# Turning x at stage borders: the norm weights applied in place in PSUM, the two parts taken four blocks at a time

## The chip, the core and the metric

The kernel runs on one core of one Trainium2 chip. The metric is the device time of one execution in microseconds (us). Before the change it is 942.28 us, the median of three runs (942.03 to 942.88).

The core's engines work side by side and meet through semaphores. TensorE (PE in the profile, with PEld for its weight loads) multiplies matrices and writes to PSUM, VectorE (DVE) and ScalarE (ACT) do elementwise work, GpSimd (POOL) does a little of it, and SyncE (SP) starts transfers.

## The reference

The kernel computes a two-layer encoder on x, 256 tokens by 1024 features. Each layer is

```
x += 0.5 * swiglu(rms_norm(x, ffn1_norm), ...)
x += mixer(rms_norm(x, mix_norm))
x += 0.5 * swiglu(rms_norm(x, ffn2_norm), ...)

rms_norm(x, g) = x * rsqrt(mean(x*x) + 1e-6) * g
swiglu(h, w_gate, w_up, w_down) = (silu(h @ w_gate) * (h @ w_up)) @ w_down
```

The mixer of the first layer holds global and windowed attention side by side; that of the second is a two-dimensional neighbourhood attention. A last norm follows. That makes six stages in a row, numbered 0 to 5: feed-forward, even mixer, feed-forward, feed-forward, odd mixer, feed-forward. Everything is float32.

## The kernel before, in words

**Three products for one.** Each float32 matrix is split into a high part in the reduced format fp32r and a low part, the rest. A product is then high times high, high times low and low times high: `mm` (lines 471 to 473) issues these three matmuls for each piece of weight, in that order: x's high part against the weight's high part (L471), x's high part against the weight's low part (L472), x's low part against the weight's high part (L473). ScalarE makes high parts (`high_part`, L479, a plain copy into fp32r) and VectorE low parts (`low_part`, L482, source minus high part). Both do so for all weights as well, which come by DMA into three raw buffers and are split some way ahead of their use into seven buffers.

**Turned x.** A matmul needs x with features on the partitions. x lies in two tiles of 128 tokens (tt = 0 and 1) by 1024 features. When a stage ends, each half row of x, 512 features, gets its last addition from VectorE (`add_to_x`, L614). Then `after` (L1392) spawns the task `prepare` (L521) for that token tile and half, and for the second half also `row_rstd` (L494), which sums the squares on ScalarE (L500, two passes) and has 1/sqrt taken. The norm's row factor is applied later, behind the matmul; the norm's weights, one for each feature, are applied while x is turned, where features lie on partitions and a weight is one scalar per partition.

`prepare` works in three steps. In the first, TensorE transposes four blocks of 128 by 128 into one PSUM bank (L527; the tag is `tp`, and there are two such banks). In the second, ScalarE makes four high parts, each by one instruction that reads a block, multiplies by the weights and writes to SBUF (`part_h`, L512; the profile calls these tiles `th`). In the third, VectorE makes four low parts, each by one instruction that reads the block again, multiplies again and takes the high part off (`part_l`, L517; tiles `tl`). I call such a set of four blocks a group. There are four groups at each border (two token tiles with two halves) and five borders, so 20 groups. Stage 0 turns its x by other code (`first_gates`), which uses `part_h` and `part_l` too.

**The order of the work.** Each engine runs its instructions in the order in which the program issues them; nothing reorders them. The program is a main line of matmuls in which every three matmuls (`mm`) are followed by a `tick` (L274). A tick advances the tasks: each `yield n` in a task means that its next step is issued n ticks later. A tick also lets the weight splitting go on, at a rate that is a table's entry for each stage. So where an instruction stands in ScalarE's or VectorE's queue is fixed by ticks that were counted when the program was built, not by what happens on the chip.

At a border the matmuls of the next stage begin with token tile 0, block by block through its eight blocks of 128 features (`project`, L602), then token tile 1. The program starts a token tile's when the steps of both its groups have all been issued (`ready`, L535). A group of the second half is thus first used by the fifth block of its `project`. In the feed-forward stages, `x_sums` (L727) also adds high and low parts together again (L738).

Of the kernel before, what the change touches and what calls it, by code (L numbers as in the profile page):

```python
# [10 lines left out]
F32R = mybir.dt.float32r  # L11
BF16 = mybir.dt.bfloat16
U16 = mybir.dt.uint16
AF = mybir.ActivationFunctionType
# [4 lines left out]
P = 128  # L19
# [3 lines left out]
KD = D // P  # L23
# [182 lines left out]
class Trunk:  # L206
# [287 lines left out]
    def row_rstd(self, tt, dest):  # L494
# [8 lines left out]
        nc.vector.tensor_tensor(s, ss[:, 0:1], ss[:, 1:2], op=ALU.add)  # L503
        dest[tt] = self.rstd(s, 1, D)[:, 0:1]

    def part_h(self, tb, tt, i, k, j):

        if (i, tt) not in self.hts:
            self.hts[i, tt] = [self.one.tile([P, KD, P], F32R, tag=f"hT{tt}{p}", name=self.name(f"t{p}")) for p in "hl"]
        hi, lo = (t[:, k, :] for t in self.hts[i, tt])  # L510
        gain = self.gains[:, i * KD + k : i * KD + k + 1]
        self.nc.scalar.activation(hi, tb[:, j * P : j * P + P], AF.Copy, scale=gain)  # L512
        return hi, lo
# [7 lines left out]
    def prepare(self, tt, i, half, dest):  # L521

        nc = self.nc
        tb = self.bank("tp")
        for j in range(4):
            b = half * 4 + j
            nc.tensor.transpose(tb[:, j * P : (j + 1) * P], self.x[tt][:, b * P : (b + 1) * P], self.ident)  # L527
        yield 1
        his = [self.part_h(tb, tt, i, half * 4 + j, j) for j in range(4)]
        yield 1  # L530
        for j, hl in enumerate(his):
            self.part_l(tb, tt, i, half * 4 + j, j, hl)
        dest += his

    def ready(self, tt):  # L535

# [1029 lines left out]
```

## Time and profile before

| of the profiled execution | value |
|---|---|
| its own time | 942.26 us |
| span of its instructions | 940.5 us |
| TensorE busy | 921.8 us, 98% |
| VectorE busy | 783.1 us, 83% |
| ScalarE busy | 677.8 us, 72% |
| GpSimd busy | 91.9 us, 10% |
| high parts of turned x, L512, by ScalarE | 96 instructions |
| low parts of turned x, L517, by VectorE | 96 instructions |
| transposes of x in `prepare`, L527 | 80 instructions |

Of the 96, 80 belong to `prepare` and 16 to stage 0. A line of the grouped view names the source line, the engine, the operation, what it writes and reads, the shape and the count; then the busy time and the mean in ns of one; then the time that the engine stood idle just before such instructions and what ended that. A line of the timeline gives start and length in us, and a number in brackets is idle time before it. Where several equal instructions follow each other they are one line with "x4", and its length runs from the first start to the last end. Matmuls are pipelined: one of 512 columns is shown with 0.39 us, but the next one starts about 0.227 us after it.

### The profile page before, as it was taken

The page shows a single profiled execution, that of the slowest core. Times are in us where ns is not written, and L with a number is a line of the kernel's source. Part 1 is how long each engine was busy: PE and PEld are TensorE (multiplying, and loading weights), DVE is VectorE, ACT ScalarE, POOL GpSimd, SP SyncE. Part 2 cuts the span into 40 slices and gives each one's busy share as a digit, 9 for nine tenths or more (in the row PEclk, how much of TensorE's full clock was granted, in tenths as well). Part 3 has the DMA queues.
Part 4 walks back from the last instruction along what each step waited for, and adds up shares of the span by engine and source line. Part 5 has one row for each costly group of instructions (what it writes and reads, how often), then busy time and mean ns, then how long its engine had stood idle before and what let it go on. Part 6 is the DMA issues. An engine that isn't in the chain of part 4 may idle for free.

```text
span 940.5 us, 12389 instructions
## 1 busy us (share of the span) xinstructions
PE 921.8 (98%) x4399; PEld 752.7 (80%) x4399; DVE 783.1 (83%) x1212; ACT 677.8 (72%) x1091; POOL 91.9 (10%) x152
## 2 busy tenths in 40 slices
PE   9999999999999999999999999999999999999997
PEld 6887888877878787888888878778878788878886
DVE  6799778778869989889978897989767687987897
ACT  7678975467787778875657778657877577769753
POOL 1300000064410000000100000008030000000001
PEclk9999999999999999999999999999999999999999
DMA  8857875554326577767466877575534358487851
GB/s 298 278 171 247 250 233 194 184 150 109 101 91 200 201 236 228 236 210 252 151 186 221 201 234 229 202 251 172 167 104 136 133 180 246 137 255 228 219 224 45
DMA packets 129343, 183.16 MB, mean 195 GB/s; under 512 B 50688, under 2 KB 63744, under 8 KB 129280
## 3 DMA queue, kind: packets, MB, share of 16 engines
q1 hardware_dynamic: 128704, 181.58, 61.2%
q10 hardware_dynamic: 576, 0.79, 0.2%
q8 instruction: 34, 0.56, 0.2%
q14 instruction: 29, 0.24, 0.1%
HBM read 169.76 MB, written 1.05 MB: 182 GB/s over the span
## 4 chain that ended last, share of the span: by engine, by line
PE 66%; DVE 16%; ACT 10%; issue 4%; DMA 3%; POOL 0%; SPq 0%; POOLq 0%; ACTq 0%; DVEq 0%
PE pj L471 9%; PE pj L472 9%; PE pj L473 9%; PE s L472 9%; PE s L473 9%; PE s L471 9%; DVE lo L482 7%; ACT hi L479 3%; DMA glu<-turned 2%; ACT turned L560 2%; DVE raw L395 2%; PE o L1040 2%; ACT shi L479 2%; PE tp L1117 1%; PE o L472 1%
## 5 line engine op out<-in xcount | busy, mean ns | idle before, releaser
L482 DVE TENSOR_TENSOR lo<-raw,hi 128x1024 fp32r<-128x1024 f32 (+1 forms) x372 | 376.1, 1031 | 78.5 <-ACT hi L479 77.0
L479 ACT ACTIVATE hi<-raw 128x1024 fp32r<-128x1024 f32 (+1 forms) x372 | 318.7, 889 | 50.3 <-DMA raw<-in_ffn_w_up 13.8
L471 PE MATMUL pj<-hi,th 128*128 128x512 f32 x367 | 146.7, 400 | 0.9 <-ACT glu L766 0.9
L472 PE MATMUL s<-lo,th 128*128 128x512 f32 x373 | 145.5, 390 | 1.0 <-DVE lo L482 1.0
L472 PE MATMUL pj<-lo,th 128*128 128x512 f32 x367 | 143.9, 392 | 2.6 <-DVE lo L482 2.3
L471 PE MATMUL s<-hi,th 128*128 128x512 f32 x373 | 146.2, 392 | 0.0
L473 PE MATMUL s<-hi,tl 128*128 128x512 f32 x373 | 145.3, 390 | 0.0
L473 PE MATMUL pj<-hi,tl 128*128 128x512 f32 x367 | 143.3, 390 | 0.0
L472 PEld LDWEIGHTS pj<-lo,th 128*128 128x128 f32 x367 | 69.1, 188 | 17.9 <-DVE lo L482 5.5
L472 PEld LDWEIGHTS s<-lo,th 128*128 128x128 f32 x373 | 70.1, 188 | 16.4 <-DVE lo L482 2.1
L473 PEld LDWEIGHTS s<-hi,tl 128*128 128x128 f32 x373 | 70.0, 188 | 14.5
L471 PEld LDWEIGHTS s<-hi,th 128*128 128x128 f32 x373 | 70.1, 188 | 14.4
L471 PEld LDWEIGHTS pj<-hi,th 128*128 128x128 f32 x367 | 69.0, 188 | 15.4 <-ACT glu L766 1.3
L473 PEld LDWEIGHTS pj<-hi,tl 128*128 128x128 f32 x367 | 68.9, 188 | 14.5
L491 POOL TENSOR_TENSOR rstd<-var,mhalf 128x1 f32<-128x1 f32 (+2 forms) x16 | 17.1, 1070 | 593.7 <-ACT th L512 314.4
L560 ACT COPY turned<-glu 128x1024 uint16<-128x1024 uint16 (+1 forms) x48 | 60.1, 1251 | 9.7 <-DMA glu<-turned 9.7
L479 ACT ACTIVATE shi<-raw 128x1024 fp32r<-128x1024 f32 x30 | 31.8, 1059 | 42.4 <-DVE raw L395 26.1
L556 ACT COPY turned<-glu 128x1024 uint16<-128x1024 uint16 (+1 forms) x48 | 46.4, 966 | 21.1 <-DVE glu L794 14.8
L471 PE MATMUL s<-hi,g_h 128*128 128x512 f32 (+1 forms) x131 | 51.4, 392 | 0.0
L473 PE MATMUL s<-hi,g_l 128*128 128x512 f32 (+1 forms) x131 | 50.9, 388 | 0.0
L472 PE MATMUL s<-lo,g_h 128*128 128x512 f32 (+1 forms) x131 | 50.8, 388 | 0.0
L479 ACT ACTIVATE shi<-two 128x1024 fp32r<-128x1024 f32 x30 | 31.7, 1057 | 19.2 <-DVE two L395 19.1
(482 smaller groups left out, 1677.3 us busy)
## 6 DMA issues: line engine op xcount, KB each, us to landing
raw<-in_ffn_w_down SPq DMA_DIRECT2D x44, 1024.0 KB, 5.1
raw<-in_ffn_w_up SPq DMA_DIRECT2D x28, 1024.0 KB, 5.3
raw<-in_ffn_w_gate SPq DMA_DIRECT2D x26, 1024.0 KB, 5.0
raw<-in_ffn_w_gate SPq DMA_DIRECT2D x35, 512.0 KB, 4.1
raw<-in_ffn_w_up SPq DMA_DIRECT2D x32, 512.0 KB, 5.1
raw<-in_odd_w_qkv SPq DMA_DIRECT2D x12, 1024.0 KB, 5.1
raw<-in_even_w_in SPq DMA_DIRECT2D x4, 1024.0 KB, 5.1
raw<-in_even_w_out SPq DMA_DIRECT2D x8, 512.0 KB, 5.8
```

The costliest lines, as they stand in the source:

```text
L395: add = lambda o, x, y: self.nc.vector.tensor_tensor(o, x, y, op=ALU.add)
L471: mm(ps, h, wh, start=first, stop=False)
L472: mm(ps, h, wl, start=False, stop=False)
L473: mm(ps, l, wh, start=False, stop=last)
L479: self.nc.scalar.activation(hi, src, AF.Copy)
L482: self.nc.vector.tensor_tensor(lo, src, hi.bitcast(F32), op=ALU.subtract)
L491: nc.gpsimd.tensor_tensor(r[:, :n], v[:, :n], self.mhalf[:, :n], op=ALU.pow)
L556: self.nc.scalar.copy(planes.rearrange("p (h c) -> p h c", h=2), back.rearrange("p (c h) -> p h c", h=2))
L560: self.nc.scalar.copy(planes.rearrange("p (c h) -> p h c", h=2), back.rearrange("p (h c) -> p h c", h=2))
L1040: self.nc.tensor.matmul(O[64 * s : 64 * s + 64, i * P : i * P + P], v(b0 + i, s, kc), pT[s][:, i, kc, :], start=(kc == 0), stop=(kc == 1),)
L1117: nc.tensor.transpose(tb[:, o : o + P], p[:, i, kc * P : kc * P + P], self.ident)
```

## The change

`prepare` alone is changed. After the transposes, ScalarE multiplies each of the four blocks by its weights and writes the product back to the same place in PSUM. One instruction of ScalarE then makes the high part of all four blocks (512 columns), and in the third step one instruction of VectorE makes the low part of all four. The number of steps and the ticks between them stay. `part_h` and `part_l` stay for stage 0, and the allocation of the tiles moves into a function of its own.

```diff
+    def turned_x(self, i, tt):
         if (i, tt) not in self.hts:
             self.hts[i, tt] = [self.one.tile([P, KD, P], F32R, tag=f"hT{tt}{p}", name=self.name(f"t{p}")) for p in "hl"]
-        hi, lo = (t[:, k, :] for t in self.hts[i, tt])
+        return self.hts[i, tt]
...
         yield 1
-        his = [self.part_h(tb, tt, i, half * 4 + j, j) for j in range(4)]
+        at = slice(half * 4, half * 4 + 4)
+        for j in range(4):
+            block, b = tb[:, j * P : (j + 1) * P], i * KD + half * 4 + j
+            nc.scalar.activation(block, block, AF.Copy, scale=self.gains[:, b : b + 1])
+        hi, lo = (t[:, at, :].rearrange("p a b -> p (a b)") for t in self.turned_x(i, tt))
+        self.high_part(hi, tb)
         yield 1
-        for j, hl in enumerate(his):
-            self.part_l(tb, tt, i, half * 4 + j, j, hl)
-        dest += his
+        self.low_part(lo, tb, hi)
+        dest += [tuple(t[:, k, :] for t in self.turned_x(i, tt)) for k in range(half * 4, half * 4 + 4)]
```

More of the change, by code (lines that the diff above doesn't have):

```diff
@@ L504, in row_rstd, with part_h @@
         dest[tt] = self.rstd(s, 1, D)[:, 0:1]
-    def part_h(self, tb, tt, i, k, j):
+    def turned_x(self, i, tt):
         if (i, tt) not in self.hts:
             self.hts[i, tt] = [self.one.tile([P, KD, P], F32R, tag=f"hT{tt}{p}", name=self.name(f"t{p}")) for p in "hl"]
-        hi, lo = (t[:, k, :] for t in self.hts[i, tt])
+        return self.hts[i, tt]
+    def part_h(self, tb, tt, i, k, j):
+        hi, lo = (t[:, k, :] for t in self.turned_x(i, tt))
         gain = self.gains[:, i * KD + k : i * KD + k + 1]
```

## The prediction

> **What bounds the kernel now.** I read the page first, for the share of each engine and the chain that ended last.
>
> ```profile
> span 940.5 us, 12389 instructions
> PE 921.8 (98%) x4399; PEld 752.7 (80%) x4399; DVE 783.1 (83%) x1212; ACT 677.8 (72%) x1091; POOL 91.9 (10%) x152
> PE 66%; DVE 16%; ACT 10%; issue 4%; DMA 3%; POOL 0%; SPq 0%; POOLq 0%; ACTq 0%; DVEq 0%
> ```
>
> TensorE is busy for all but 18.7 us of the span. The change touches no matmul, so it can change the time only by a wait of TensorE that it creates or removes. The next question is whether TensorE waits for turned x today. The answers for the low parts of turned x and for TensorE's waits, longest first, say:
>
> ```profile
> L517 DVE SCALAR_TENSOR_TENSOR tl<-tp,mats,th x88: 335/343/352, 5.3 to 765.5; 128x128 fp32r<-128x128 f32 x88
> who waited for it (us, times):
> busy tenths in 40 slices 2000000110011000000200000002000020000000
> PE pj L472 <- DVE lo L482: 2.3, 3, 0.9
> ```
>
> Nothing stands under "who waited for it": no engine ever waited for a low part of turned x, and the longest wait of TensorE, 2.3 us in all, is for weights. The stretches around the three borders into feed-forward stages agree: TensorE is busy for the whole of each (19.00 of 19.00, 17.00 of 17.00).
>
> ```profile
> 273.00:292.00 19.00, 19.00 (x105) 15.83 (x102) 17.24 (x35) 17.01 (x35) 2.05 (x2) 1.00 0.45 144
> 451.00:470.00 19.00, 19.00 (x93) 15.71 (x92) 17.17 (x37) 15.37 (x33) 2.96 (x2) 1.00 0.43 137
> 753.00:770.00 17.00, 17.00 (x84) 14.17 (x83) 14.73 (x31) 15.25 (x32) 1.10 (x2) 1.00 0.43 134
> ```
>
> The fourth and fifth numbers of busy time are VectorE's and ScalarE's. So at the borders there is nothing to win, and the question is whether the cover of turned x is thick enough for what the change adds on ScalarE.
>
> **What one group costs, before and after.** These rows carry the prices:
>
> ```profile
> L512 ACT ACTIVATE th<-tp,mats 128x128 fp32r<-128x128 f32 x88 | 25.2, 371 | 26.5 <-PE tp L527 24.1 <-PE tp L633 2.3
> L517 DVE SCALAR_TENSOR_TENSOR tl<-tp,mats,th 128x128 fp32r<-128x128 f32 x88 | 25.1, 343 | 12.5 <-ACT th L512 12.5
> L1015 ACT ACTIVATE pt<-tp 128x512 f32<-128x512 f32 x32 | 18.9, 595 | 4.9 <-PE tp L1117 4.7
> L482 DVE TENSOR_TENSOR oqT<-tp,oqT 64x512 fp32r<-64x512 f32 x8 | 5.5, 689 | 2.4 <-ACT oqT L479 2.2
> L715 DVE TENSOR_TENSOR quarters<-quarters 128x128 f32<-128x128 f32 x15 | 4.4, 292 | 0.5
> 220.55 0.60 ACT L1015 ACTIVATE pt<-tp 128x512 f32<-128x512 f32 x1
> 221.05 0.47 ACT L1095 ACTIVATE p<-s,m 128x256 f32<-128x256 f32 x1
> ```
>
> Here are the groups of the border into stage 3, ScalarE's four, two of VectorE's rows, and the two matmuls that first use the last group's high part (L471) and low part (L473):
>
> ```profile
> 452.26 1.15 ACT L512 ACTIVATE th<-tp,mats 128x128 fp32r<-128x128 f32 x4 [6.95 <-PE tp L527]
> 456.58 1.11 ACT L512 ACTIVATE th<-tp,mats 128x128 fp32r<-128x128 f32 x4
> 458.67 1.14 ACT L512 ACTIVATE th<-tp,mats 128x128 fp32r<-128x128 f32 x4
> 462.04 1.12 ACT L512 ACTIVATE th<-tp,mats 128x128 fp32r<-128x128 f32 x4
> 462.98 1.23 DVE L482 TENSOR_TENSOR lo<-raw,hi 128x1024 fp32r<-128x1024 f32 x1
> 464.12 1.12 DVE L517 SCALAR_TENSOR_TENSOR tl<-tp,mats,th 128x128 fp32r<-128x128 f32 x4
> 465.80 0.39 PE L471 MATMUL s<-hi,th 128*128 128x512 f32 x1
> 466.25 0.39 PE L473 MATMUL s<-hi,tl 128*128 128x512 f32 x1
> ```
>
> Before, a group of four takes ScalarE 1.14 us; one lasts 0.371, so the starts are (1.14 - 0.37)/3, about 0.255 us, apart. The next instruction can start about 0.255 after the fourth, 1.02 after the first. VectorE's four take about 1.12.
>
> After, four in-place passes and one pass over 512 columns. No row shows ScalarE writing to PSUM. I take the in-place pass as the present one, 0.371 long at a step of 0.255, since only the destination differs. The wide high part reads what the four wrote, so I expect it to wait for the fourth to end. The one case in the rows of such a wait within an engine is L715, which uses what the instruction before it wrote and comes 0.5/15, about 0.035 us, after idle time. Then the wide pass starts 0.765 + 0.371 + 0.035 = 1.17 after the first, lasts 0.595 (L1015, PSUM to SBUF, the same size), and the next instruction starts 0.50 after it (220.55 to 221.05). That is 1.67 against 1.02: each group holds ScalarE for e = 0.655 us more, and its own high part is ready 1.77 after its start instead of 1.14, 0.63 later. Over 20 groups ScalarE gets 13.1 us more. VectorE does one instruction of 0.69 in place of four in 1.12, so 20 x 0.43, about 8.6 us less.
>
> From a group's start to its low part: before, 1.14 + 0.04 + 1.12 = 2.30 where VectorE is free; after, 1.77 + 0.04 + 0.69 = 2.50. A single group is hardly later. What counts is that all of it stands in ScalarE's queue in a fixed order, so that the extra time of a border's groups adds up until ScalarE next stands idle. Queued behind the groups are the sums of squares, high parts of weights and, in feed-forward stages, the first silu; nothing is moved past them, and no transfer is moved.
>
> I follow that sum to the last group of each border, the latest there. At the border into stage 3 only 0.03 us of idle time lies between the groups (458.67 follows the transposes). The last high part ends before at 463.16, and after at 463.16 + 3e + 0.63 - 0.03 = 465.73. TensorE wants it at 465.80: met. The low part ends at 465.73 + 0.73 = 466.46; TensorE wants it at 466.25: **0.2 us late**. VectorE itself is free by then: the weight's low part ahead of it (462.98), whose high part is 3e later, ends about 465.3.
>
> The other two borders into feed-forward stages (stages 2 and 5):
>
> ```profile
> 280.81 1.14 ACT L512 ACTIVATE th<-tp,mats 128x128 fp32r<-128x128 f32 x4 [1.00 <-PE tp L527]
> 283.39 1.15 ACT L512 ACTIVATE th<-tp,mats 128x128 fp32r<-128x128 f32 x4
> 287.00 0.39 PE L473 MATMUL s<-hi,tl 128*128 128x512 f32 x1
> 759.98 1.15 ACT L512 ACTIVATE th<-tp,mats 128x128 fp32r<-128x128 f32 x4 [0.92 <-PE tp L527]
> 762.56 1.15 ACT L512 ACTIVATE th<-tp,mats 128x128 fp32r<-128x128 f32 x4
> 766.17 0.39 PE L473 MATMUL s<-hi,tl 128*128 128x512 f32 x1
> ```
>
> Here 1.00 and 0.92 us of idle time lie ahead of the third group and take up most of the first two groups' 2e. Into stage 2 the last low part ends at 284.54 + (2e - 1.00) + e + 0.63 + 0.73 = 286.87 against 287.00, into stage 5 at 763.72 + (2e - 0.92) + e + 0.63 + 0.73 = 766.13 against 766.17. Both are met, by 0.13 and 0.04 us. The borders into the mixers:
>
> ```profile
> 188.96 1.14 ACT L512 ACTIVATE th<-tp,mats 128x128 fp32r<-128x128 f32 x4 [0.79 <-PE tp L527]
> 192.18 1.14 ACT L512 ACTIVATE th<-tp,mats 128x128 fp32r<-128x128 f32 x4 [0.18 <-PE tp L527]
> 196.54 0.39 PE L473 MATMUL s<-hi,tl 128*128 128x512 f32 x1
> 639.79 1.14 ACT L512 ACTIVATE th<-tp,mats 128x128 fp32r<-128x128 f32 x4 [0.79 <-PE tp L527]
> 643.08 1.15 ACT L512 ACTIVATE th<-tp,mats 128x128 fp32r<-128x128 f32 x4
> 647.84 0.39 PE L473 MATMUL pj<-hi,tl 128*128 128x512 f32 x1
> ```
>
> The same sum gives 193.32 + 3e + 0.63 - 0.97 + 0.73 = 195.68 against 196.54, and 644.23 + 3e + 0.63 - 0.79 + 0.73 = 646.77 against 647.84: 0.86 and 1.07 us to spare.
>
> **The sum** is 0.2 us of new waiting, at one border. What follows the borders absorbs the rest: the weights' high parts behind the groups are for buffers that TensorE has only just freed, and ScalarE, which is 1.6 to 2.6 us late after a border (4e less the idle time), soon stands idle; after the border into stage 2 that is for 3.15 us:
>
> ```profile
> 296.26 1.06 ACT L479 ACTIVATE hi<-raw 128x1024 fp32r<-128x1024 f32 x1 [3.15 <-PE pj L473]
> ```
>
> So no weight is later when TensorE wants it. VectorE's saved time is worth nothing at the borders, where TensorE waits for nothing. The profiled execution took 942.26 us, 0.02 from the median, so I forecast **942.5 us**.
>
> **Bounds of the unknown price**, the in-place pass. From below: a faster destination; once e falls under 0.60, the wait of 0.2 is gone too, and the time is 942.3. No gain beyond that is possible at a border, since no wait stands there. From above: within one bank the pass may have to read and then write. 384 columns more cost (0.50 - 0.255) = 0.245 us, so a second stretch of 128 columns costs 0.08 each; four times this is 0.33, and e is 0.98. Higher still: each pass waits for the one before it to end, 0.405 apart instead of 0.255, which gives e = 1.10. I take the present pass's own price, as the row nearest in all but the destination.
>
> The Trainium skill, page "ScalarE: Activation LUTs", section "Step-by-step: what each stage is for", says that ScalarE writes to PSUM with less latency than to SBUF. By that rule the time would be the 942.3 of the lower bound. No row of this profile shows ScalarE writing there, so the trace neither bears it out nor speaks against it.
>
> **The rivals.**
>
> *No new wait at all* (942.3). The in-place pass is shorter than 0.371, or the wide pass does not wait for the fourth to end; either takes e under 0.60. For it: the margin at the border into stage 3 is a matter of 0.06 us in e. Against it: L715's gap. It cannot be told from my forecast by the time.
>
> *ScalarE becomes the bound at the borders* (slower). If the in-place pass reads and writes one after the other, e is 0.98, and each 4e counts at the last group: the low parts come 1.5 us late into stage 3, 1.2 into stage 2, 1.3 into stage 5, 0.4 into stage 1 and 0.2 into stage 4, in all 4.6: 946.9. With e = 1.10 the waits are 2.0, 1.6, 1.7, 0.9 and 0.7, together 6.9: 949.2. It decides from about e = 0.81 on, where the three feed-forward borders add up to 1.9 us, 0.2% of the time; that is 0.04 us more per in-place pass than I assume. For it: reading and writing one bank in one instruction is shown by no row. Against it: the transposes' bank is used by nothing else meanwhile, and 0.255 per pass of 128 columns against 0.245 for 384 columns more shows that most of a short pass is a fixed cost, under which a second stretch could hide.
>
> *VectorE's saved time shortens later waits* (faster). It has 4 x 0.43 = 1.7 us less at each border, and TensorE's largest waits are for low parts of weights. But between a border and those waits the engines stand idle (3.15 us above), so the saving is lost before it gets there. Were the 2.3 us of the first row of waits to vanish, the time would be 940.0; more likely by far is a third of it at most, 941.5.
>
> **How the numbers follow.** 0.2% of the time, 1.9 us, is about what a measurement of this kernel can tell from no change; that puts "same" between 940.4 and 944.2. My forecast (0.2 us of waiting, or the little that e around 0.655 makes of it) has a chance of 0.52 and the rival without any wait 0.28. ScalarE as the bound gets 0.15, of which a fifth is e so little over 0.655 that the time stays under 944.2. VectorE's gain gets 0.05, of which I leave 0.03 to gains over 1.9 us. So slower is 0.12, faster 0.03, same 0.85. The range reaches from 941.5, the gain that I allow VectorE, to 944.6, about e = 0.845 by the three borders' sum (2.3 us); the rest of the slow rival, about 0.1, and the tail of the gains lie outside.
>
> **What would show it.** If I am right, the profile after has 80 ScalarE rows of 128x128 from PSUM to PSUM near 371 ns, 20 of 128x512 near 595 and 20 of VectorE near 690; ScalarE's busy time is some 12 us higher and VectorE's some 14 lower (a sum of lengths: 80 x 0.343 less 20 x 0.69); the list of TensorE's waits has at most some tenths of a us for turned x, at the border into stage 3; the border stretches stay full. A ScalarE group of over 1.93 us instead of 1.77 up to the end of the wide pass, with TensorE's gaps before the fifth block of token tile 1 at all three feed-forward borders, would show the slow rival. A time under 940 with fewer waits for weights' low parts would show VectorE's.

## The result and the profile after

The changed kernel takes 950.51 us (median of five runs, 950.37 to 951.81) against 942.12 us for the kernel before in the same comparison: a ratio of 1.009, 95% interval 1.0078 to 1.0101. It is 8.4 us slower. The prediction said 942.5 us, between 941.5 and 944.6.

The page's first lines and its shares of the chain, for the kernel after (span, then busy time of each engine):

```profile
span 949.1 us, 12346 instructions
PE 925.5 (98%) x4399; PEld 751.4 (79%) x4399; DVE 775.8 (82%) x1152; ACT 692.8 (73%) x1111; POOL 90.5 (10%) x152
PE 59%; DVE 17%; ACT 14%; issue 4%; DMA 4%; POOL 0%; SPq 0%; POOLq 0%; ACTq 0%; DVEq 0%
```

The span grew by 8.6 us and TensorE's busy time by only 3.7. Its work is no slower: matmuls of 512 columns start 227 ns apart in both traces. So the loss is in new waits of TensorE. ScalarE is busy 15.0 us longer (12 were forecast). Of VectorE the prediction gave a sum of lengths, 14 us less, and it came: the low parts of turned x shrink by 13.6, from 80 x 0.343 to 13.8. The page counts overlapping lengths once, so its busy time falls by only 7.3, near the 20 x 0.43 = 8.6 that the prediction has for that. In the chain, TensorE fell from 66% to 59%, while ScalarE rose from 10% to 14%: it now decides more often when things happen, though it stands idle for a quarter of the span.

The groups of the change, from the grouped view of the kernel after (count, then busy time and mean ns, then idle time before it):

```profile
L535 ACT ACTIVATE tp<-tp,mats 128x128 f32<-128x128 f32 x80 | 27.1, 339 | 22.2 <-PE tp L530 20.2
L479 ACT ACTIVATE th<-tp 128x512 fp32r<-128x512 f32 x20 | 12.0, 598 | 0.6
L482 DVE TENSOR_TENSOR tl<-tp,th 128x512 fp32r<-128x512 f32 x20 | 13.8, 690 | 20.6 <-ACT th L479 20.6
```

Each single length is what the prediction took or shorter: 339 ns for an in-place pass instead of 371, 598 and 690 ns for the wide parts. The lengths do not show what is wrong. The starts do. These are the first group of the border into stage 3, the pass after it, and the last group of that border with TensorE's and VectorE's rows that hang on it, from the timeline of the kernel after:

```profile
455.74 1.46 ACT L535 ACTIVATE tp<-tp,mats 128x128 f32<-128x128 f32 x4 [6.59 <-PE tp L530]
457.23 0.60 ACT L479 ACTIVATE th<-tp 128x512 fp32r<-128x512 f32 x1
457.73 0.62 ACT L500 ACTIVATE sq<-x 128x512 f32<-128x512 f32 x1
...
468.21 1.44 ACT L535 ACTIVATE tp<-tp,mats 128x128 f32<-128x128 f32 x4
469.69 0.60 ACT L479 ACTIVATE th<-tp 128x512 fp32r<-128x512 f32 x1
470.32 0.69 DVE L482 TENSOR_TENSOR tl<-tp,th 128x512 fp32r<-128x512 f32 x1 [0.75 <-ACT th L479]
470.34 0.50 PE L471 MATMUL s<-hi,th 128*128 128x512 f32 x1 [0.74 <-ACT th L479]
471.06 0.50 PE L473 MATMUL s<-hi,tl 128*128 128x512 f32 x1
```

Four in-place passes span 1.46 us, each 0.339 long, so they start (1.46 - 0.339)/3 = 0.374 us apart: each waits for the one before it to end (0.339), and 0.035 more. The passes before, which wrote to SBUF, started 0.255 apart and overlapped. A group now holds ScalarE from 455.74 to 457.73, 1.99 us instead of 1.02. The prediction's e, the extra time of ScalarE per group, is 0.97 us and not 0.655. In the compiled program the cause can be read: the second, third and fourth in-place pass and the wide pass each wait on a semaphore that ScalarE itself raises when the pass before is done. Passes into different SBUF columns carry no such wait.

The last rows show the price: TensorE stands for 0.74 us at 470.34 waiting for a high part. TensorE's list of waits (total us, times, longest), which before had no row for turned x:

```profile
PE tp L472 <- DVE slo L482: 2.1, 2, 1.3
PE tp L530 <- DVE x L621: 1.8, 2, 1.5
...
PE tp L556 <- ACT nat L1336: 1.6, 1, 1.6
...
PE s L471 <- ACT th L479: 0.7, 1, 0.7
```

Turned x itself (`th`) accounts for 0.7 us. The large new rows are for other things: `slo`, the low part of a summed weight matrix, rose from 0.8 to 2.1 us, and `nat`, the scaled keys of the odd mixer, is new with 1.6.

Where the time comes in is seen best by matching TensorE's 4399 instructions of the two traces one to one (their order is the same) and following how much later each starts. The lag changes at a few places only:

| place (us in the trace before) | lag grows by, us | TensorE's instruction there |
|---|---|---|
| first 11 us | 0.56 | start of the program; -0.4 to 0.6 from run to run |
| 196 to 199, border into stage 1 | 0.31 | low parts of turned x |
| 211 | 0.15 | in the attention, `s<-kTbz,qTb` |
| 280 to 287, border into stage 2 | 1.14 | transposes 0.44, a weight's low part 0.52, turned x 0.18 |
| **312.6, inside stage 2** | **1.54** | `tp<-slo,k14h`, a weight's low part |
| 369 | -0.23 | a wait for a weight's low part, shorter than before |
| 460 to 467, border into stage 3 | 1.50 | high parts 1.02, low parts and the rest 0.48 |
| 470 to 640 | -0.07 | several places |
| 642, border into stage 4 | 0.32 | transposes |
| **646.2, stage 4** | **1.78** | transposes of the scaled keys `nat` |
| 760 to 773, border into stage 5 | 1.62 | a weight's low part 0.71, turned x 0.41, weights' low parts 0.50 |

The sum is 8.6 us. The five borders together are 4.9; two waits well behind a border add 3.3.

The stretches around the borders into stages 2 and 3, from the view of busy time by windows, to hold against the full ones of before (TensorE, weight loads, VectorE, ScalarE, GpSimd):

```profile
275.00:294.00 19.00, 18.50 (x88) 14.76 (x87) 13.09 (x21) 18.20 (x37) 1.11 (x2) 1.00 0.38 116
455.00:474.00 19.00, 18.26 (x87) 14.22 (x86) 13.81 (x22) 17.65 (x37) 2.03 (x2) 1.00 0.34 112
```

At the first, ScalarE was busy for 17.01 of 19 us and is now for 18.20, nearly all. VectorE fell from 17.24 to 13.09: it now stands behind ScalarE.

**How a late ScalarE reaches stage 2's inside.** From the timelines at the border into stage 2, first the kernel before (the prediction has its last group, at 283.39):

```profile
284.56 1.28 ACT L672 ACT_TABLE_LOAD   x1
287.53 1.23 DVE L482 TENSOR_TENSOR lo<-raw,hi 128x1024 fp32r<-128x1024 f32 x1 [0.34 <-ACT hi L479]
...
311.24 1.22 DVE L482 TENSOR_TENSOR slo<-two,shi 128x1024 fp32r<-128x1024 f32 x1
```

and the kernel after:

```profile
288.25 1.28 ACT L679 ACT_TABLE_LOAD   x1
291.21 1.22 DVE L482 TENSOR_TENSOR lo<-raw,hi 128x1024 fp32r<-128x1024 f32 x1 [1.26 <-ACT hi L479]
...
314.92 1.22 DVE L482 TENSOR_TENSOR slo<-two,shi 128x1024 fp32r<-128x1024 f32 x1
316.20 0.50 PE L472 MATMUL tp<-slo,k14h 128*128 128x512 f32 x1 [1.26 <-DVE slo L482]
```

One number runs through all three pairs. The table load behind the last group is 3.69 us later, VectorE's next low part of a weight 3.68, and the `slo` of 24 us further on still 3.68, while TensorE's lag is 2.16 up to there. In the kernel before, the window from that low part on shows VectorE nearly full:

```profile
287.50:312.50 25.00, 25.00 (x112) 20.61 (x110) 23.50 (x30) 19.41 (x25) 0.00 (x0) 1.00 0.61 189
```

Of 25 us it is busy for 23.50, and behind the first low part its few idle times are the same in both traces; it has nothing with which to catch up. TensorE had a wait of 0.8 for that `slo` before, so nothing cushions it, and there its lag grows from 2.16 to 3.70, about ScalarE's and VectorE's lateness.

**How it reaches stage 4's keys.** ScalarE's scaling of the first keys and TensorE's first use of them, the kernel before and the kernel after:

```profile
644.60 0.72 ACT L1329 ACTIVATE nat<-pj,rstd 128x512 f32<-128x512 f32 x1
646.24 0.38 PE L549 MATMUL tp<-mats,nat 128*128 128x128 f32 x2
```

```profile
651.43 0.60 ACT L479 ACTIVATE th<-tp 128x512 fp32r<-128x512 f32 x1
...
652.45 0.68 ACT L1336 ACTIVATE nat<-pj,rstd 128x512 f32<-128x512 f32 x1
653.18 0.66 PE L556 MATMUL tp<-mats,nat 128*128 128x128 f32 x4 [1.57 <-ACT nat L1336]
```

The keys' scaling stands behind all four groups in ScalarE's queue. It starts 7.85 us later, 2.6 more than TensorE's own lag of 5.22 at that point. Before, it ended at 645.32 and was wanted at 646.24: 0.9 us of slack, and the other 1.7 is a new wait.

### The profile page after: what moved, and what is told of

Its sections match the earlier page's. It is cut to its first block, busy times and chain, and to the rows that moved or that the text cites. A ratio compares the mean times of both kernels' runs of the same rounds, so it can differ in the third digit from the quotient of the medians.

```text
span 949.1 us, 12346 instructions
## 1 busy us (share of the span) xinstructions
PE 925.5 (98%) x4399; PEld 751.4 (79%) x4399; DVE 775.8 (82%) x1152; ACT 692.8 (73%) x1111; POOL 90.5 (10%) x152
## 4 chain that ended last, share of the span: by engine, by line
PE 59%; DVE 17%; ACT 14%; issue 4%; DMA 4%; POOL 0%; SPq 0%; POOLq 0%; ACTq 0%; DVEq 0%
PE pj L471 8%; PE pj L472 8%; PE pj L473 8%; PE s L473 8%; PE s L472 8%; PE s L471 8%; DVE lo L482 7%; ACT hi L479 4%; ACT tp L535 2%; ACT turned L567 2%; DMA glu<-turned 2%; DVE raw L395 2%; PE o L1047 2%; DVE two L395 1%; PE tp L1124 1%
## 5 line engine op out<-in xcount | busy, mean ns | idle before, releaser
L491 POOL TENSOR_TENSOR rstd<-var,mhalf 128x1 f32<-128x1 f32 (+2 forms) x16 | 14.8, 924 | 604.5 <-DVE var L489 429.5
```

The lines of the kernel that those rows point to most:

```text
L491: nc.gpsimd.tensor_tensor(r[:, :n], v[:, :n], self.mhalf[:, :n], op=ALU.pow)
```

## The experiments

My theory after the result was that ScalarE's longer groups are the whole cause: at the borders, and through the queues behind them. The main rivals were VectorE's wide low part, which can start only when all four blocks are done; that the forecast's e would have been free; and the in-place writes to PSUM as such. In the expectations, A is on the side of ScalarE's added time, and the rivals are named there. The kernel before was run beside each: 941.91 us for *narrow_low*, *wide_low*, *dose1* and *dose1_wide*; 942.70 for *only2*, *only4*, *only135* and *to_sbuf*; 942.92 for *nosum_before*, *nosum_only2*, *pad* and *vector_gain*; 942.70 for *dose097* and *nat_later*.

**narrow_low: the kernel after, with VectorE's four small low parts back.**

```diff
-        self.low_part(lo, tb, hi)
+        for j in range(4):
+            part = slice(j * P, (j + 1) * P)
+            self.low_part(lo[:, part], tb[:, part], hi[:, part])
```

> ScalarE as in the changed kernel (four in-place passes, one wide high part), but VectorE makes the low part by four instructions of 128 columns instead of one of 512. Theory A (the loss comes from ScalarE's extra time per group, and a later low part only adds to it): VectorE is back near 1.1 us per group instead of 0.69, the last group's low part is about 0.4 us later at four of the five borders, so 950.5 + 1 to 2 = 951.5 to 952.5 us. Theory B (the loss comes from the width: the first of four blocks must wait for an instruction over all four): narrow low parts can be used one by one, so 948 to 950 us.

Measured 950.57 us, ratio 1.0092 (1.0077 to 1.0107), the time of the kernel after. Neither number given was met. The four small parts take VectorE 0.88 us per group here and not 1.12, as each is now a plain subtraction, so this run tests only 0.19 us of the 0.43; *wide_low* tests the whole. Within that, VectorE's wide instruction is neither a help nor a harm.

**wide_low: the kernel before, with VectorE's low part of four blocks in one instruction.**

```diff
-        for j, hl in enumerate(his):
-            self.part_l(tb, tt, i, half * 4 + j, j, hl)
+        hi, lo = (t[:, half * 4 : half * 4 + 4, :].rearrange("p a b -> p (a b)") for t in self.hts[i, tt])
+        self.low_part(lo, tb, hi)
```

> ScalarE as before the change (four narrow high parts with the weights, nothing in place), VectorE with one wide low part per group; that low part leaves out the norm's weights, so the output differs. Theory A: no extra time on ScalarE, nothing is late: 942.1 within 0.5 us, and VectorE's saved time (20 x 0.43 us) is worth nothing. Theory B (width): slower by 1 to 3 us. Theory C (VectorE's saved time shortens later waits): faster, 939 to 941 us.

Measured 941.89 us, ratio 1.0000 (0.999 to 1.0009). VectorE's saving, had by itself (the low parts then lack the norm's weights, which changes no length), is worth nothing.

**dose1: the kernel before, with one needless ScalarE pass of 512 columns ahead of each group; dose1_wide: that and the wide low part, without the weights as in wide_low.**

```diff
...
+        for _ in range(1):
+            self.high_part(self.hts[i, tt][0][:, half * 4 : half * 4 + 4, :].rearrange("p a b -> p (a b)"), tb)
         his = [self.part_h(tb, tt, i, half * 4 + j, j) for j in range(4)]
```

> The kernel before with one more ScalarE pass over 512 columns per group, ahead of the four narrow high parts; VectorE as before. Theory A: as the run before, plus low parts about 0.43 us later at the three feed-forward borders: 944 to 946 us. If VectorE's saved time is worth nothing in either, both runs differ by under 0.5 us.

> As the run with the wide low part (weights left out in the low part), and ScalarE makes one more pass over 512 columns per group ahead of the four narrow high parts, which overwrite it. That is the ScalarE time that the prediction assumed (about 0.6 us more per group) without the four waits of in-place passes. Theory A as the prediction had it (only lateness at a border's last group counts): 942.5. Theory A with what it left out (turned x late passes on through VectorE's full queue into the weights of stage 2, and through ScalarE's queue to the first keys of stage 4): about 0.2 + 0.9 + 0.7 = 1.8 more than before, 943 to 945 us.

Measured 944.62 us, 1.0030 (1.0019 to 1.0041), and 945.24 us, 1.0038 (1.0023 to 1.0053). The timeline of *dose1*, first group into stage 3:

```profile
453.45 0.60 ACT L479 ACTIVATE th<-tp 128x512 fp32r<-128x512 f32 x1 [6.86 <-PE tp L527]
454.08 1.15 ACT L512 ACTIVATE th<-tp,mats 128x128 fp32r<-128x128 f32 x4
455.10 0.65 ACT L500 ACTIVATE sq<-x 128x512 f32<-128x512 f32 x1
```

The added pass costs 0.63 us, so e is very nearly the 0.655 of the forecast. With it the forecast's own sum gives 0.1 to 0.2 us; the chip loses 2.7. The steps of TensorE's lag show where: 0.7 at the border into stage 2, 0.8 at `slo`, 0.8 at `nat`, 0.3 at the border into stage 5, and no step of 0.2 or more into stage 3, where the forecast saw its only wait. The forecast was thus wrong by two independent errors, the size of e and the waits that it did not follow.

**dose097: a pass of 512 and one of 128 columns ahead of each group of the kernel before; nothing is written in place.**

```diff
...
+        spare = self.hts[i, tt][0][:, half * 4 : half * 4 + 4, :].rearrange("p a b -> p (a b)")
+        self.high_part(spare, tb)
+        self.high_part(spare[:, 0:P], tb[:, 0:P])
         his = [self.part_h(tb, tt, i, half * 4 + j, j) for j in range(4)]
```

> The kernel before with two more ScalarE passes per group ahead of the four narrow high parts, one over 512 and one over 128 columns, so that a group holds ScalarE about 0.97 us longer, as in the changed kernel, with nothing in place in PSUM. Theory A (only the time that a group holds ScalarE's queue counts): 950.5 within 1 us. Rival (writing in place in PSUM, or the one wide high part, has a cost of its own): under 948 us.

Measured 950.88 us, 1.0085 (1.007 to 1.01). Its timeline, and its waits of TensorE:

```profile
455.26 0.91 ACT L479 ACTIVATE th<-tp 128x512 fp32r<-128x512 f32 x2 [6.18 <-PE tp L527]
456.20 1.14 ACT L512 ACTIVATE th<-tp,mats 128x128 fp32r<-128x128 f32 x4
457.22 0.65 ACT L500 ACTIVATE sq<-x 128x512 f32<-128x512 f32 x1
```

```profile
PE tp L472 <- DVE slo L482: 1.9, 2, 1.1
PE tp L554 <- ACT nat L1334: 1.5, 1, 1.5
```

A group holds ScalarE for 1.96 us, e = 0.94, and the time is that of the kernel after, with the same two large waits. ScalarE's time per group accounts for the whole loss within the noise, without any write to PSUM. The places share it out otherwise: TensorE's lag grows by 0.8 us in the attention of stage 1, at 206 to 211 us, where the kernel after has 0.3 at the border and 0.15 there, and by 1.1 instead of 1.5 into stage 3. The dose and the loss together: e of 0.63 costs 2.7 us, 0.94 costs 8.2, 0.97 costs 8.4. Past the margins the loss grows much faster than e.

**only2, only4, only135: the change at some borders only** (into stage 2, into stage 4, into the other three).

```diff
+        wide = i in (2,)
+        if wide:
+            ...
+            return
         his = [self.part_h(tb, tt, i, half * 4 + j, j) for j in range(4)]
```

> The change at the border into stage 2 alone; the other four borders as before. In the trace of the changed kernel TensorE falls behind by about 1.1 us at this border and by another 1.5 us some 30 us later, before a matmul that waits for the low part of a weight sum. Theory A (that later wait is the same lateness, carried on by VectorE's full queue): both parts stay, 2.4 to 2.8 us over the kernel before. Rival (the later wait comes from lateness gathered at earlier borders or from other places): about 1.1 us.

> The change at the border into stage 4 (odd mixer) alone. Theory A: TensorE waits 0.3 to 0.4 us at the transposes and 1.6 to 1.8 us before it turns the first keys, whose scaling stands behind the groups in ScalarE's queue: 2.0 to 2.2 us over the kernel before. Rival (that wait is for something that is late from before): under 0.6 us.

> The change at the borders into stages 1, 3 and 5. Theory A: only late turned x and late weights at these borders, no long wait behind them: 0.3 to 0.6 at the first, 1.0 to 1.3 at the second, 1.4 to 1.7 at the third, together 2.8 to 3.6 us over the kernel before. With the two runs above, the three sum up to the changed kernel's 8.4 within 0.8 us if borders act on their own; under 6 or over 10 if they act on each other.

Measured 945.83 us (1.0030; 1.0019 to 1.0041), 945.26 us (1.0030; 1.0018 to 1.0042) and 946.63 us (1.0043; 1.0027 to 1.0059). Over the kernel before that is 3.1, 2.6 and 3.9 us, 9.6 in all against 8.4. In the profiled run of *only135* the granted clock was 0.89 between 625 and 640 us, which adds some 1.6 us to that execution and has nothing to do with the edit. The steps of TensorE's lag, taken without it, add up: 2.7 us in *only2* (1.14 at the border, 1.56 at `slo`), 2.1 in *only4* (0.25 at transposes, 1.84 at `nat`) and 3.4 in *only135*. That is 8.2 against the 8.1 that the kernel after shows behind its first 11 us. Left out of these sums are waits of the first transposes of a border for VectorE's last addition to x, at 451.6 and 632.7 us of the trace before. They stand ahead of the change's first instruction at that border, and the one at 632.7 grows by 0.1 to 0.4 us in most runs, in *wide_low* and *nosum_before* too, which have ScalarE's work as before. They make up some of the 9.6. Each border's cost is its own, and over half of what the borders into stages 2 and 4 cost arises behind them.

**nosum_before and nosum_only2: the kernel before and *only2*, each without the four additions on VectorE in which stage 2 sums parts of turned x.** This tests whether VectorE's full queue carries the lateness to `slo`.

```diff
-                nc.vector.tensor_tensor(o, x, y, op=op)
+                if self.now.n != 2:
+                    nc.vector.tensor_tensor(o, x, y, op=op)
```

> The kernel before, leaving out in stage 2 four VectorE instructions of 0.55 us (the differences of sums of turned x for the seven-product scheme; the output differs). It is the base for the next run. VectorE's queue in stage 2 is 2.2 us shorter ahead of the waits of 1.4 us at 314 to 319 us: 940.5 to 942 us.

> The change at the border into stage 2 alone, with the same four VectorE instructions left out. Theory A (the wait 30 us behind the border is lateness that VectorE's full queue carries on): with 2.2 us of room in that queue the later wait of 1.5 us is gone, and only the border's own 1.1 us stays: 0.8 to 1.5 us over the run before. Rival (it is carried by something else, such as a transfer or ScalarE): 2.4 to 3.2 us over it.

Measured 942.82 us (0.9998; 0.9987 to 1.0008) and 943.77 us (1.0001; 0.9991 to 1.0012). TensorE's wait there, first in *only2*, then in *nosum_only2*:

```profile
PE tp L472 <- DVE slo L482: 2.1, 2, 1.3
```

```profile
PE tp L472 <- DVE slo L482: 0.8, 1, 0.8
```

The wait falls back to the 0.8 that the kernel before and *nosum_before* have, the step at 312 us is gone, and the change at this border costs 0.95 us by the medians, and 1.2 by TensorE's lag between the two traces, instead of 3.1. With some room in its queue VectorE does catch up. So the step at `slo` is carried by VectorE, as the timelines suggested.

**nat_later: the kernel after, with the transposes of the first keys three ticks later.**

```diff
+            late = 3 if i == 1 and tt == 0 and not groups else 0
...
-            yield NAT_WAIT
+            yield NAT_WAIT + late
```

> The changed kernel, with one edit: in the odd mixer the turning of the first keys of token tile 0 is issued three ticks (some 2 us of matmuls) later. Theory A (TensorE's 1.8 us there are a wait at the head of its queue for a ScalarE result that is late by that much, and nothing else needs the keys so early): 948.5 to 949.5 us. Rival (the lateness goes on to the next consumer): 950 us or more.

Measured 950.55 us, 1.0081 (1.0064 to 1.0098). The row for `nat` is gone from TensorE's waits, and of the step at 646 us 0.4 is left. But the time is only about 0.5 us better over its kernel before than the kernel after was (7.85 against 8.39), which the intervals do not separate; in its profiled run the transposes ahead of that place waited longer instead:

```profile
PE tp L530 <- DVE x L621: 2.7, 2, 2.5
```

That wait lies ahead of the edit's place: there this execution lost 1.0 us that the kernel after did not. How much of the 1.8 us a later use of the keys brings back stays open.

**to_sbuf and pad: the four passes into SBUF instead of in place, and a control.** The wide parts then read the product in SBUF. Room for the product (one 128x512 tile, `flat`) came from keeping the discarded squares as bytes. *pad* is the kernel before with only these changes of scratch memory; `flat` is there but holds no more than the zeros of the start.

```diff
-            nc.scalar.activation(block, block, AF.Copy, scale=self.gains[:, b : b + 1])
+            nc.scalar.activation(flat[:, j * P : (j + 1) * P], block, AF.Copy, scale=self.gains[:, b : b + 1])
...
-            sq = self.one.tile([P, 512], F32, tag="sq", name=self.name("sq"))
+            sq = self.one.tile([P, 512], mybir.dt.uint8, tag="sq16", name=self.name("sq"))
...
-        zeros = one.tile([P, 512], F32, tag="sq", name="zeros")
+        zeros = one.tile([P, 512], F32, tag="flat", name="zeros")
...
-        self.mhalf = self.little([P, FILLER], "mhalf")
+        self.mhalf = self.little([P, 8], "mhalf")
```

> As the changed kernel, but the four passes with the weights write to one buffer in SBUF instead of back to their place in PSUM, and the wide high and low parts read that buffer. (For room, the discarded squares of the sum of squares are kept as bytes.) Theory A: the passes start 0.255 us apart again instead of 0.375, only the wide pass remains as extra ScalarE time, about 0.65 us per group, and the time is that of the runs with one more wide pass, 944 to 946 us. Rival (the passes' step is a cost of reading and working through four blocks, wherever they go): 950 us.

> The kernel before with the memory places of the run that passes through SBUF and nothing else of it: the discarded squares are kept as bytes, and the 2 KB buffer is there but holds only the zeros of the start. In that run the matmuls whose weights are parts of the gated products came 231 to 235 ns apart instead of 227, all through the program. Theory L (that comes from where the tiles lie in SBUF): 947 to 950 us here as well, so that the passes through SBUF themselves cost 3 to 5 us. Rival (it comes from the passes): 942 us.

Measured 952.85 us, 1.0109 (1.0088 to 1.013), and 948.14 us, 1.0048 (1.003 to 1.0066). The timeline of *to_sbuf*:

```profile
457.82 1.15 ACT L537 ACTIVATE flat<-tp,mats 128x128 f32<-128x128 f32 x4 [7.09 <-PE tp L530]
458.99 0.63 ACT L479 ACTIVATE th<-flat 128x512 fp32r<-128x512 f32 x1
459.53 0.61 ACT L500 ACTIVATE sq<-x 128x512 uint8<-128x512 f32 x1
```

Out of PSUM the passes are back at the old step: four span 1.15 us, the group takes 1.71, and e is 0.69. The four passes of a group there carry no wait for each other. So the wait from pass to pass comes with writing back to the tile that is read; what would happen without the semaphore, or with each block in a bank of its own, was not tried. Yet *to_sbuf* is slower than the kernel after, and *pad*, with no change to the work, loses 5.2 us. The grouped rows of TensorE show it, first of the kernel before, then of *pad*:

```profile
L471 PE MATMUL pj<-hi,g_h 128*128 128x512 f32 x73 | 28.4, 389 | 0.0
L472 PE MATMUL pj<-lo,g_h 128*128 128x512 f32 x73 | 28.4, 389 | 0.0
L473 PE MATMUL pj<-hi,g_l 128*128 128x512 f32 x73 | 28.4, 389 | 0.0
```

```profile
L471 PE MATMUL pj<-hi,g_h 128*128 128x512 f32 x73 | 28.7, 393 | 0.0
L472 PE MATMUL pj<-lo,g_h 128*128 128x512 f32 x73 | 29.0, 397 | 0.0
L473 PE MATMUL pj<-hi,g_l 128*128 128x512 f32 x73 | 28.9, 396 | 0.0
```

Matmuls on parts of the gated product (`g_h`, `g_l`) are 4 to 8 ns longer, and start 231 to 235 ns apart on average instead of 227; there are 927 of them with 512 columns, which at some 6.3 ns each makes 5.8 us, against 5.6 between the two spans. In the kernel after they stand at 227 ns, so none of its 8.4 us comes from this. Without it, *to_sbuf* costs 952.85 - 948.14, about 4.7 us. That is more than *dose1*'s 2.7 for nearly the same e; against *pad*, its lag grows by 1.1 at `slo` and 1.4 at `nat`. One further wait shows in it: the one tile `flat` must be read by VectorE before ScalarE may fill it again, 0.7 us in all. What the rest is stays open.

**vector_gain: the weights applied by VectorE, four blocks in one instruction, in place; ScalarE makes the wide high part alone.**

```diff
-        for j in range(4):
-            block, b = tb[:, j * P : (j + 1) * P], i * KD + half * 4 + j
-            nc.scalar.activation(block, block, AF.Copy, scale=self.gains[:, b : b + 1])
+        blocks = tb.rearrange("p (a b) -> p a b", a=4)
+        b = i * KD + half * 4
+        gain = self.gains[:, b : b + 4].unsqueeze(2).to_broadcast([P, 4, P])
+        nc.vector.tensor_tensor(blocks, blocks, gain, op=ALU.mult)
```

> The weights applied in place by VectorE, all four blocks in one instruction (the weights spread along each block), then one wide high part by ScalarE and one wide low part by VectorE. ScalarE's busy time per group falls from about 1.02 to 0.50 us, VectorE's rises from 1.04 to 1.25. Theory A (what counts is how long a group holds ScalarE's queue, waits within it too): ScalarE must stand until VectorE has come to the group and taken 0.69 us, 1.2 us or more from the transposes on, so 943 to 946 us. Rival (what counts is ScalarE's busy time): at or below 942 us.

Measured 958.03 us, 1.0151 (1.0135 to 1.0167), far beyond what was expected. Its groups:

```profile
L479 ACT ACTIVATE th<-tp 128x512 fp32r<-128x512 f32 x20 | 12.0, 598 | 53.0 <-DVE tp L536 53.0
L536 DVE TENSOR_TENSOR tp<-tp,mats 128x512 f32<-128x512 f32 x20 | 13.8, 692 | 1.5 <-PE tp L530 1.5
```

ScalarE has less work than before the change (667.0 us busy, from its page) and is later than ever: it stands idle for 53.0 us with its queue behind a high part, waiting for VectorE, whose multiplication is behind other work in VectorE's queue. TensorE waits for high parts of turned x for 4.6 us and for the keys for 2.7. The time that ScalarE spends waiting at the head of its queue holds up what is behind it just as its work does.

None of these kernels beat the one before the change.

## Why the prediction was wrong

**The step of the in-place pass was mis-sized.** The prediction took "a step of 0.255, since only the destination differs". It measured 0.374, because the passes wait for each other; that is the prediction's own far bound ("each pass waits for the one before it to end"), at 0.339 + 0.035 in place of 0.371 + 0.035. The choice went by the row nearest in kind, the present pass, and missed that the new passes read and write one PSUM tile, so that the program makes each wait for a semaphore of the one before. The prediction did assume such a wait for the wide pass, so the question was asked once and not four times. e became 0.97 instead of 0.655 (the terms of the prediction make 0.651, which changes nothing), and the sign that it named, a group of over 1.93 us up to the end of the wide pass, is there: 2.09.

**The rule on PSUM writes held and did not decide.** The Trainium skill, page "ScalarE: Activation LUTs", section "Step-by-step: what each stage is for", has writes to PSUM faster than to SBUF. The trace agrees: 339 ns against 371, and against 364 in *to_sbuf*, where the output is plain float32 too. The 942.3 us that would follow did not, since shorter passes that no longer overlap come more slowly one after the other.

**The sum over the last groups was nearly right for the e that came.** For e = 0.98 the slow rival gave 1.5, 1.2, 1.3, 0.4 and 0.2 us into stages 3, 2, 5, 1 and 4, together 4.6. The lag grew by 1.50, 1.14, 1.62, 0.31 and 0.32, together 4.9. In part that is luck. The rival had its 0.98 from another mechanism, a pass that reads and then writes, and not from a wait between passes. And into stages 2 and 5 more than half of it came at transposes and weights' low parts, which wait for VectorE's additions to x and its low parts of weights, both later because ScalarE is, and not at the last group that the prediction followed. VectorE's rows into stage 2 show it, in the kernel after:

```profile
280.24 0.69 DVE L482 TENSOR_TENSOR tl<-tp,th 128x512 fp32r<-128x512 f32 x1 [1.63 <-ACT th L479]
280.85 0.68 DVE L621 SCALAR_TENSOR_TENSOR x<-pj,x 128x512 f32<-128x512 f32 x1
```

The low part waits for ScalarE, and the addition to x behind it starts 2.54 us later than before; the transposes that follow at 281.58 need it.

**"What follows the borders absorbs the rest" failed, and so did "no weight is later when TensorE wants it".** The argument rested on one idle time of ScalarE, 3.15 us at 296.26. ScalarE does recover there, but VectorE had by then taken over the lateness and had no idle time to give back: 1.54 us at `slo`, shown by the runs without sums. At the border into stage 4 the scaled keys, which are not in the prediction's list of what is queued behind the groups, had 0.9 us of slack and came 2.6 late: 1.7 us. These two, 3.3 us by the lag, 0.3 at the borders and 0.4 in all at the remaining places, the start above all, are the difference between the slow rival's 946.9 and the profiled 950.86. *dose1* shows that the step fails with the forecast's own e as well, where it costs 2.5 us more than the forecast.

**VectorE's saving is worth nothing: right.** *wide_low* and *narrow_low* show it from both sides. That TensorE waits nowhere for turned x before the change, so nothing can be won at a border, was right too.

**The chances.** The slow rival got 0.15 because 0.81 for e seemed far from 0.655. It was 0.04 us per pass away, as the text itself said, on a price that no row showed.

## What to carry to other kernels

Price an added instruction by the distance between starts, and ask of each pair of neighbours whether the program makes the second wait for the first, as it did here for passes that read and write one tile; then a shorter instruction can still cost more time. When an in-order engine becomes later, list all that is queued behind it and follow the lateness into the engine that it feeds until that engine stands idle, not only until the first one does. Here an engine that was busy for 94% of a stretch passed a delay on in full, 24 us later.

## What the runs showed of the hardware

- ScalarE's passes in place in one PSUM bank, each behind a semaphore of the one before: 339 ns long, 374 ns from start to start. Into SBUF, without such waits: 364 to 371 ns long, 255 ns from start to start.
- The layout of scratch tiles in SBUF changed the speed of matmuls: the same 942 us program with a few tiles made smaller or added (*pad*) lost 5.2 us, with matmuls on parts of the gated product starting 231 to 235 ns apart instead of 227. That the place of these parts does it is inferred, as the traces hold no addresses; which property of the place was not tried.
